# FFN gate and up of a hybrid encoder layer by seven products of halves in place of eight

## The chip, the cores and the metric

The kernel runs on one core of one Trainium2 chip. The metric is the device time in microseconds of one execution. Before: a median of 2740.31 us over 3 runs (2740.05 to 2740.49).

## What is computed

One encoder layer on 512 tokens of width 2048, in float32: a Hyena branch (long convolution) and a grouped-query attention branch, gated and merged, an output projection, and a SwiGLU feed-forward block of width 5632. The change touches the last two steps:

```python
    x = x + merged @ w_out
    h2 = rms_norm(x, ffn_norm_g)
    return x + (jax.nn.silu(h2 @ w_ffn_gate) * (h2 @ w_ffn_up)) @ w_ffn_down
```

## The kernel before

Activations lie with channels on the 128 partitions and the 512 tokens on the free axis, so a layer's input is 16 tiles of 128x512. Every weight product is taken in three matmuls (`mm3`): weights and activations are split exactly into a high and a low part, and high x high, low x high and high x low are added in one PSUM bank of 128x512. Weights come from one packed array in tiles of eight 128x128 blocks (512 KB), in the order of `weight_blocks`. `wblk` loads a tile on SP's queue (L152), casts its high part on ScalarE (L153) and subtracts it on VectorE for the low part (L154). There are 2 buffers of raw tiles and 3 each of highs and lows. All matmuls are recorded in L104, in program order; the order on the other engines is made by a scheduler.

`group` sums one 128-row output tile over its input tiles. The output projection runs 16 groups o; each adds the input (L689), and splits x2 times the norm's gain into x2h and x2l (L692, L693); `sumsq_add` gathers the squares. The norm's factor per token is not applied to x2: `token_rstd` makes it (rs2) as queued side work between matmuls and spreads it over the partitions in rbc, and gate and up are multiplied by it. Its chain is four matmuls rs2ss, a square root on ScalarE, some small VectorE steps, rs2dg, and four matmuls rs2bcp.

The feed-forward block goes in three chunks of the 44 tiles of 128 hidden channels (`DOWN`). For each tile a gate group fg and an up group fu of 48 matmuls each are followed by two scalings, Silu, a product and a split into act (L715 to L719, L176); after each chunk, 16 groups d of the down projection are added to x2 in SBUF (L725), and after the last the result is stored (L727).

Of the kernel before, what the change touches and what calls it, by code (L numbers as in the profile page):

```python
# [829 lines left out]
```

## Time and profile before

| | |
|---|---|
| median of 3 runs | 2740.31 us |
| span of the profiled execution, first to last instruction | 2738.6 us |
| TensorE busy | 2726.2 us, 12358 matmuls |
| weight loads busy (beside the matmuls) | 2250.8 us |
| VectorE busy | 1119.4 us |
| ScalarE busy | 789.8 us |
| read from HBM | 257.90 MB |

The profiled execution is one run with the hardware profiler on. A row of a group reads: line, engine, operation, written tile, read tiles, shapes, count, then busy time, mean length of one in ns, and the engine's idle time just ahead of them with what ended it. A row of a timeline reads: start and length in us, engine, line, operation, tiles, and in brackets the idle time ahead of it. The matmul records overlap, since matmuls are pipelined; what a matmul costs is the distance from start to start. A row of windows reads: the stretch, its length, then busy time and count for TensorE, weight loads, VectorE, ScalarE and GpSimd, the granted TensorE clock, the DMA share and GB/s. PEld is the weight load, SPq and ACTq are queues that issue DMAs.

### The profile page before, as it was taken

To read this page: it belongs to the slowest core of one execution; us is meant where nothing else is said; L and a number is where in the kernel's file an instruction comes from. 1 tells how busy PE (TensorE), PEld (TensorE's weight loads), DVE (VectorE), ACT (ScalarE), POOL (GpSimd) and SP (SyncE) were. 2 spreads that over 40 slices of the span, in tenths; PEclk is the share of its full clock that TensorE was granted. 3 is DMA by queue.
4 is the path that set the end of the run, shared out by engine and by line. 5 is a ranking of instruction groups with operands and counts; after the bars stand their busy time and mean duration, and the time that the engine had idled before them with its cause. 6 is when DMAs were issued, how large, how long until landed. Compare 5 with 4: busy or idle time off the path is not lost.

```text
span 2738.6 us, 29658 instructions
## 1 busy us (share of the span) xinstructions
PE 2726.2 (100%) x12358; PEld 2250.8 (82%) x12358; DVE 1119.4 (41%) x1520; ACT 789.8 (29%) x1098; POOL 34.7 (1%) x70
## 2 busy tenths in 40 slices
PE   9999999999999999999999999999999999999999
PEld 7777888888888888888888888888888888888887
DVE  7666654675333334434333332323333332333332
ACT  6333323565222223233222221222222212222221
POOL 0000001110000000000000000000000000000000
PEclk9999999999999999999999999999999999999999
...
GB/s 201 79 71 72 66 62 112 70 61 63 100 94 99 98 95 100 154 100 95 97 93 100 96 96 100 93 100 94 99 98 94 100 93 100 97 96 100 92 127 96
DMA packets 77763, 264.02 MB, mean 96 GB/s; under 512 B 8667, under 2 KB 9627, under 8 KB 77628
## 3 DMA queue, kind: packets, MB, share of 16 engines
...
HBM read 257.90 MB, written 4.19 MB: 96 GB/s over the span
## 4 chain that ended last, share of the span: by engine, by line
PE 98%; DVE 1%; ACT 1%; DMA 0%; issue 0%; SPq 0%; DVEq 0%
PE fg L104 17%; PE fu L104 17%; PE d L104 17%; PE g L104 13%; PE px L104 7%; PE o L104 6%; PE b L104 6%; PE phv L104 3%; PE q L104 2%; PE kv L104 2%; PE kp L104 2%; PE ab L104 1%; PE up L104 1%; PE av L104 1%; PE sp L104 1%; PE fp L104 1%
## 5 line engine op out<-in xcount | busy, mean ns | idle before, releaser
L153 ACT CAST wh<-wr 128x1024 fp32r<-128x1024 f32 (+1 forms) x467 | 489.4, 1049 | 1661.5 <-PE d L104 369.1
L154 DVE TENSOR_TENSOR wl<-wr,wh 128x1024 fp32r<-128x1024 f32 (+1 forms) x467 | 568.2, 1217 | 800.1 <-ACT wh L153 799.3
L104 PE MATMUL fu<-x2h,wh 128*128 128x512 f32 x704 | 274.0, 389 | 0.0
L104 PE MATMUL fg<-x2h,wh 128*128 128x512 f32 x704 | 274.0, 389 | 0.0
L104 PE MATMUL fu<-x2h,wl 128*128 128x512 f32 x704 | 273.9, 389 | 0.0
L104 PE MATMUL fg<-x2h,wl 128*128 128x512 f32 x704 | 273.9, 389 | 0.0
L104 PE MATMUL fg<-x2l,wh 128*128 128x512 f32 x704 | 273.9, 389 | 0.0
L104 PE MATMUL fu<-x2l,wh 128*128 128x512 f32 x704 | 273.9, 389 | 0.0
L104 PE MATMUL g<-xh,wh 128*128 128x512 f32 x512 | 200.4, 391 | 0.0
L104 PE MATMUL g<-xh,wl 128*128 128x512 f32 x512 | 199.4, 390 | 0.0
L104 PE MATMUL g<-xl,wh 128*128 128x512 f32 x512 | 199.4, 389 | 0.0
L104 PEld LDWEIGHTS fu<-x2l,wh 128*128 128x128 f32 x704 | 132.1, 188 | 27.5
L104 PEld LDWEIGHTS fg<-x2l,wh 128*128 128x128 f32 x704 | 132.1, 188 | 27.5
L104 PEld LDWEIGHTS fu<-x2h,wh 128*128 128x128 f32 x704 | 132.1, 188 | 27.4
L104 PEld LDWEIGHTS fg<-x2h,wh 128*128 128x128 f32 x704 | 132.1, 188 | 27.4
L104 PEld LDWEIGHTS fu<-x2h,wl 128*128 128x128 f32 x704 | 132.1, 188 | 27.4
L104 PEld LDWEIGHTS fg<-x2h,wl 128*128 128x128 f32 x704 | 132.1, 188 | 27.4
L104 PEld LDWEIGHTS g<-xh,wl 128*128 128x128 f32 x512 | 96.1, 188 | 20.1
L104 PE MATMUL px<-xh,wh 128*128 128x512 f32 x272 | 109.9, 404 | 2.5 <-ACT xh L408 1.3
L104 PEld LDWEIGHTS g<-xh,wh 128*128 128x128 f32 x512 | 96.1, 188 | 19.4
L104 PEld LDWEIGHTS g<-xl,wh 128*128 128x128 f32 x512 | 96.1, 188 | 19.2
L104 PE MATMUL px<-xh,wl 128*128 128x512 f32 x272 | 106.4, 391 | 0.5 <-DVE wl L154 0.5
...
## 6 DMA issues: line engine op xcount, KB each, us to landing
wr<-wpk SPq DMA_DIRECT2D x463, 512.0 KB, 3.3
xr<-xT SPq DMA_DIRECT2D x16, 256.0 KB, 5.6
x<-xT ACTq DMA_DIRECT2D x16, 256.0 KB, 5.2
out<-x SPq DMA_DIRECT2D x16, 256.0 KB, 2.4
dec<-decT ACTq DMA_DIRECT2D x8, 256.0 KB, 2.7
T<-tbl POOLq DMA_DIRECT2D x8, 256.0 KB, 5.1
wr<-wpk SPq DMA_DIRECT2D x4, 128.0 KB, 3.7
w<-w ACTq DMA_DIRECT2D x4, 128.0 KB, 2.6
```

The costliest lines, as they stand in the source:

```text
L104: tc.keep_in_program_order(nc.tensor.matmul(out, lhsT=lhsT, rhs=rhs, start=start, stop=stop, **kw))
L153: nc.scalar.copy(hi[:, c], raw[:, c])
L154: nc.vector.tensor_tensor(lo[:, c], raw[:, c], hi[:, c].bitcast(F32), ALU.subtract)
```

## The change

Gate and up now take two output tiles (j, j+1) of one of the two weights at a time, a group n of 44. The product is written as 2x2 halves: the weights by output tile and by even or odd input tile (a11, a12, a21, a22, each one packed tile of eight blocks), the activations by even or odd input tile and by the first or second 256 tokens. In place of eight products of halves, seven are made, of sums of halves (the Winograd form of Strassen's scheme).

- Weights: four VectorE sums a group (s1, s2, s3, s4, L775), and seven splits (cast L781, subtraction L782). Raw tiles rotate through six slots.
- Activations: once, during and behind the output projection, for each pair of input tiles the seven 256-token operands (`x_sums`) and their split (`x_split`) into X. Five of the eight pairs are made while the output projection runs, the last three behind it.
- `product`: per pair of input tiles one matmul of the weight highs with 512 columns (activation highs beside lows) and one of the weight lows with 256 columns, into the second half of the same bank. A group is 7 x 8 x 2 = 112 matmuls; the two groups that it replaces had 96.
- PSUM: banks fx (two slots), fy and fz (one each) and three others. Products are added in a bank while earlier states of it are folded out (v1, v5, v16: the halves of the bank added by ScalarE and VectorE), so a later product on the same bank waits for the fold. The order on TensorE is A11 (fx), S1 (fy), S2 (fx), S4 (fy), S3 (fx), A12 (fz), A22 (fx); in group 0 A11, A12 and S1 come first, interleaved by pairs.
- Group 0 also runs the norm's rs2ss and rs2bcp with nothing between them, between S2 and S4.
- The first four act tiles stay in SBUF, the others go to DRAM through GpSimd's queue and come back by ScalarE's queue for the down projection. x2 goes to DRAM too and is added at the end; the down sums are gathered unscaled in dacc and multiplied by rbc2 in the last chunk. Chunks are now 12, 16 and 16, and in the first chunk the first four down groups are run side by side over the act tiles.
- A small pad and a wider tile for the negated gains shift addresses, so that the large operands start at the same place in 512 bytes.

The stages ahead of the output projection have the same instructions in the same order.

```diff
-DOWN = (16, 16, 12)
+DOWN = (12, 16, 16)
+WIDE = 4
+EARLY_ACTS = 4
+NEARLY = 5
...
+    def quadrant(name, half, j):
+        return [(name, k * P, j * P, P) for k in range(half, KT, 2)]
+    for j in range(0, FT, 2):
+        for name in ("w_ffn_gate", "w_ffn_up"):
+            for half, c in ((0, 0), (0, 1), (1, 1), (1, 0)):
+                out += quadrant(name, half, j + c)
     f0 = 0
     for n in DOWN:
-        for j in range(f0, f0 + n):
-            out += cols("w_ffn_gate", j * P, KT) + cols("w_ffn_up", j * P, KT)
-        for m in range(KT):
+        first = WIDE if f0 == 0 else 0
+        for k in range(n if first else 0):
+            out += [("w_ffn_down", (f0 + k) * P, m * P, P) for m in range(first)]
+        for m in range(first, KT):
             out += cols("w_ffn_down", m * P, n, k0=f0)
...
+    r2.release()
+    r3.release()
+    H = 256
+    NP = KT // 2
+    SQ = 7 * H
+    pad = tc.alloc_tile_pool(name="pad", bufs=1, side="right")
+    pad_t = pad.tile([P, 112], F32, name="pad_t")
+    nc.vector.memset(pad_t, 0.0)
+    wq = tc.alloc_tile_pool(name="wq", bufs=1, side="right", reuse_waits="tile")
+    xa = tc.alloc_tile_pool(name="xa", bufs=1, side="right", reuse_waits="tile")
+    vp = tc.alloc_tile_pool(name="vp", bufs=1, side="right", reuse_waits="tile")
+    def ev(name):
+        return wq.tile([P, H], F32, tag="ev", bufs=6, name=name)
+    nffg = cpool.tile([P, P], F32, name="nffg")
+    nc.vector.tensor_scalar(nffg[:, :KT], prm[:, PC["ffng"]:PC["ffng"] + KT], -1.0, None, ALU.mult)
...
+    NRAW = 6
+    raws = {"n": 0, "base": None}
+    late = {}
+    def raw_tile(i, name):
+        n = raws["n"] % NRAW
+        raws["n"] += 1
+        if n < 2:
+            t = wpool.tile([P, BLK * P], F32, tag="raw", bufs=2, name=name)
+        elif n < NRAW - 1:
+            t = wq.tile([P, BLK * P], F32, tag="rb", bufs=NRAW - 3, name=name)
+        else:
+            t = late["rc"].tile([P, BLK * P], F32, tag="rc", bufs=1, name=name)
+        nc.sync.dma_start(t, wpk[i])
+        return t
...
+    def x_sums(p, xe, xo):
+        V = vp.tile([P, SQ], F32, tag="V", bufs=3, name=f"V{p}")
+        b12 = ev(f"b12{p}")
+        v = [V[:, i * H:(i + 1) * H] for i in range(7)]
+        ge, go, ngo = pcol("ffng", 2 * p), pcol("ffng", 2 * p + 1), nffg[:, 2 * p + 1:2 * p + 2]
+        nc.scalar.activation(v[0], xe[:, :H], AF.Copy, scale=ge)
+        nc.scalar.activation(b12, xe[:, H:], AF.Copy, scale=ge)
+        nc.vector.tensor_tensor(v[2], b12, v[0], ALU.subtract)
+        nc.scalar.activation(v[1], xo[:, :H], AF.Copy, scale=go)
+        nc.scalar.activation(v[5], xo[:, H:], AF.Copy, scale=ngo)
+        nc.vector.scalar_tensor_tensor(v[4], v[5], -1.0, b12, ALU.mult, ALU.subtract)
+        nc.vector.scalar_tensor_tensor(v[3], v[4], -1.0, v[0], ALU.mult, ALU.subtract)
+        nc.vector.scalar_tensor_tensor(v[6], v[3], -1.0, v[1], ALU.mult, ALU.subtract)
+        return V
+    def x_split(p, V, cuts):
+        pool = xa if p < NEARLY else late["xb"]
+        X = pool.tile([P, 2 * SQ], F32R, tag="X", bufs=NEARLY if p < NEARLY else NP - NEARLY, name=f"X{p}")
+        X4 = X.rearrange("p (i h t) -> p i h t", i=7, h=2)
+        V3 = V.rearrange("p (i t) -> p i t", i=7)
+        for a, b in zip(cuts, cuts[1:]):
+            nc.scalar.copy(X4[:, a:b, 0, :], V3[:, a:b])
+            nc.vector.tensor_tensor(X4[:, a:b, 1, :], V3[:, a:b], X4[:, a:b, 0, :].bitcast(F32), ALU.subtract)
+        xs[p] = X
+    def wsum(name, a, b):
+        t = late["sg"].tile([P, BLK * P], F32, tag="sg", bufs=3, name=name)
+        nc.vector.tensor_tensor(t, a, b, ALU.add)
+        return t
+    def wsplit(w, name):
+        hi = wpool.tile([P, BLK * P], F32R, tag="whi", bufs=3, name=f"wh{name}")
+        lo = wpool.tile([P, BLK * P], F32R, tag="wlo", bufs=3, name=f"wl{name}")
+        nc.scalar.copy(hi, w)
+        nc.vector.tensor_tensor(lo, w, hi.bitcast(F32), ALU.subtract)
+        return hi, lo
+    def product(bank, hl, i, first, p0=0, p1=NP):
+        hi, lo = hl
+        for p in range(p0, p1):
+            c = slice(p * P, (p + 1) * P)
+            x = xs[p][:, i * 2 * H:(i + 1) * 2 * H]
+            mm(bank, hi[:, c], x, first and p == 0, False, skip_group_check=True)
+            mm(bank[:, H:], lo[:, c], x[:, :H], False, p == NP - 1, skip_group_check=True)
+    def fold(name, b):
+        t = ev(name)
+        nc.scalar.copy(t, b[:, :H])
+        nc.vector.tensor_tensor(t, b[:, H:], t, ALU.add)
+        return t
...
+    def x2_tile(m, op):
+        xt = tmp(f"x2{m}")
+        nc.scalar.dma_start(xt, xT[m])
+        nc.vector.tensor_tensor(xt, op, xt, ALU.add)
+        nc.gpsimd.dma_start(x2d[m], xt)
+        return xt
+    def bank(b, n):
+        return psf.tile([P, S], F32, tag=b, bufs=2 if b == "x" else 1, name=f"f{b}{n}")
+    xt = []
+    V = {}
     for m in range(KT):
...
+        xt.append(x2_tile(m, op))
+        if m % 2:
+            p = m // 2
+            if p < NP - 1:
+                V[p] = x_sums(p, xt[m - 1], xt[m])
+            if p < NEARLY:
+                x_split(p, V[p], (0, 7))
+        if m < KT - 1:
+            sumsq_add(acc2, xt[m], m, "x2sq")
+    raws["base"] = state["tile"]
+    psm.release()
+    psf = tc.alloc_tile_pool(name="psf", bufs=1, space=PSUM, reuse_waits="tile")
+    w0 = group_raws(0)
+    h11 = wsplit(w0["a11"], "a11_0")
+    x, y, z = (bank(b, 0) for b in "xyz")
+    product(x, h11, 0, True, 0, NEARLY)
+    h12 = wsplit(w0["a12"], "a12_0")
+    product(z, h12, 1, True, 0, NEARLY)
+    r1.release()
+    late["sg"] = tc.alloc_tile_pool(name="sgp", bufs=1, reuse_waits="tile")
+    late["xb"] = tc.alloc_tile_pool(name="xb", bufs=1, reuse_waits="tile")
+    s1 = wsum("s1_0", w0["a21"], w0["a22"])
+    hs1 = wsplit(s1, "s1_0")
+    product(y, hs1, 2, True, 0, NEARLY)
+    V[NP - 1] = x_sums(NP - 1, xt[-2], xt[-1])
+    for p in range(NEARLY, NP):
+        x_split(p, V[p], (0, 3, 7))
+        product(x, h11, 0, True, p, p + 1)
+        product(z, h12, 1, True, p, p + 1)
+        product(y, hs1, 2, True, p, p + 1)
+    sumsq_add(acc2, xt[-1], KT - 1, "x2sq")
+    vp.release()
...
     rbc2 = cpool.tile([P, S], F32, tag="bc", bufs=1, name="rbc2")
...
+    def finish(n, c):
+        j, up = n // 2 * 2, n % 2
+        if not up:
+            for t in c:
+                nc.vector.tensor_tensor(t, t, rbc2, ALU.mult)
+                nc.scalar.activation(t, t, AF.Silu)
+            gated[j] = c
+            return
+        for i, (t, g) in enumerate(zip(c, gated.pop(j))):
+            nc.vector.tensor_tensor(t, t, g, ALU.mult)
+            if j + i < EARLY_ACTS:
+                act_split(j + i, t, ea, EARLY_ACTS)
+            else:
+                nc.gpsimd.dma_start(actd[j + i], t)
+    for n in range(FT):
+        if n > 0:
+            w0 = group_raws(n)
+            x, y, z = (bank(b, n) for b in "xyz")
+            product(x, wsplit(w0["a11"], f"a11_{n}"), 0, True)
+        c0, c1 = (tmp(f"c{i}_{n}") if n % 2 else cp.tile([P, S], F32, tag="c", bufs=4, name=f"c{i}_{n}")
+                  for i in range(2))
+        v1 = fold(f"v1_{n}", x)
+        if n > 0:
+            s1 = wsum(f"s1_{n}", w0["a21"], w0["a22"])
+            product(y, wsplit(s1, f"s1_{n}"), 2, True)
+        v5 = fold(f"v5_{n}", y)
+        s2 = wsum(f"s2_{n}", s1, w0["a11"])
+        product(x, wsplit(s2, f"s2_{n}"), 3, False)
+        v16 = fold(f"v16_{n}", x)
+        if n == 0:
+            for _ in token_rstd(acc2, "rs2", {"bc": rbc2}):
+                pass
+        s4 = wsum(f"s4_{n}", s2, w0["a12"])
+        product(y, wsplit(s4, f"s4_{n}"), 5, False)
+        nc.vector.tensor_tensor(v16, v16, y[:, :H], ALU.subtract)
+        nc.vector.tensor_tensor(c0[:, H:], v16, y[:, H:], ALU.subtract)
+        s3 = wsum(f"s3_{n}", w0["a11"], w0["a21"])
+        product(x, wsplit(s3, f"s3_{n}"), 4, False)
+        nc.vector.tensor_tensor(v5, v5, x[:, :H], ALU.subtract)
+        nc.vector.tensor_tensor(c1[:, H:], v5, x[:, H:], ALU.subtract)
+        if n > 0:
+            product(z, wsplit(w0["a12"], f"a12_{n}"), 1, True)
+        nc.vector.tensor_tensor(v1, z[:, :H], v1, ALU.add)
+        nc.vector.tensor_tensor(c0[:, :H], z[:, H:], v1, ALU.add)
+        product(x, wsplit(w0["a22"], f"a22_{n}"), 6, False)
+        d = ev(f"d_{n}")
+        nc.scalar.activation(d, x[:, :H], AF.Copy, scale=-1.0)
+        nc.vector.tensor_tensor(c1[:, :H], d, x[:, H:], ALU.subtract)
+        finish(n, (c0, c1))
...
+    def act_load(j, pool, bufs):
+        t = tmp(f"actr{j}")
+        nc.scalar.dma_start(t, actd[j])
+        act_split(j, t, pool, bufs)
+    dacc = [None] * KT
+    def down(ci, f0, n, m, dp, done=False):
+        last = ci == len(DOWN) - 1
+        if ci == 0:
+            dacc[m] = r3.tile([P, S], F32, tag="r", bufs=16, name=f"dacc{m}")
+        if last:
+            x2t = tmp(f"x2r{m}")
+            nc.scalar.dma_start(x2t, x2d[m])
+            nc.vector.tensor_tensor(dacc[m], dacc[m], rbc2, ALU.mult)
+            nc.vector.tensor_tensor(dacc[m], dacc[m], x2t, ALU.add)
+        if not done:
+            group(dp, [acts[j] for j in range(f0, f0 + n)])
+        if ci == 0:
+            nc.scalar.copy(dacc[m], dp)
+        elif not last:
+            nc.vector.tensor_tensor(dacc[m], dacc[m], dp, ALU.add)
+        else:
+            t = tmp(f"dt{m}")
+            nc.vector.tensor_tensor(t, dp, rbc2, ALU.mult)
+            nc.vector.tensor_tensor(dacc[m], dacc[m], t, ALU.add)
+            nc.sync.dma_start(out[m], dacc[m])
...
+        if ci == 0:
+            for j in range(EARLY_ACTS, n):
+                act_load(j, r1, NA)
+            dps = [ps_tile(f"d0{m}") for m in range(WIDE)]
+            for k in range(n):
+                for dp in dps:
+                    wh, wl = wblk()
+                    mm3(dp, wh, wl, acts[k][0], acts[k][1], k == 0, k == n - 1)
+            for m in range(WIDE):
+                down(ci, f0, n, m, dps[m], True)
+        elif ci == 1:
+            for p in (ea, xa, wq):
+                p.release()
+            r1e = tc.alloc_tile_pool(name="r1e", bufs=1, side="right", reuse_waits="tile")
+            for j in range(f0, f0 + n):
+                act_load(j, r1e, 24)
+        else:
+            for j in range(f0, f0 + n):
+                act_load(j, r1e if j < f0 + 8 else r1, 24 if j < f0 + 8 else NA)
+        for m in range(WIDE if ci == 0 else 0, KT):
+            down(ci, f0, n, m, ps_tile(f"d{ci}{m}"))
         f0 += n
```

More of the change, by code (lines that the diff above doesn't have):

```diff
@@ new lines, in fold, with group_raws @@
+    def fold(name, b):
[3 more added lines that the diff above has]
+        return t
+    def group_raws(n):
+        b = raws["base"] + 4 * n
+        t = {}
+        for q, name in ((0, "a11"), (3, "a12"), (1, "a21"), (2, "a22")) if n == 0 else \
+                ((0, "a11"), (1, "a21"), (2, "a22"), (3, "a12")):
+            t[name] = raw_tile(b + q, f"{name}_{n}")
+        return t
+    def bank(b, n):
+        return psf.tile([P, S], F32, tag=b, bufs=2 if b == "x" else 1, name=f"f{b}{n}")
@@ L684, in layer_kernel @@
+    xt = []
+    V = {}
     for m in range(KT):
[L685 to L686 removed]
+        if m == KT - 1:
+            raws["base"] = state["tile"]
         op = ps_tile(f"o{m}")
         group(op, ms)
[L689 to L692 removed]
@@ new lines, in layer_kernel, with act_tile, act_split @@
+    late["rc"] = tc.alloc_tile_pool(name="rcp", bufs=1, reuse_waits="tile")
+    cp = tc.alloc_tile_pool(name="cp", bufs=1, reuse_waits="tile")
+    ea = tc.alloc_tile_pool(name="ea", bufs=1, side="right", reuse_waits="tile")
+    rbc2 = cpool.tile([P, S], F32, tag="bc", bufs=1, name="rbc2")
+    acts = {}
+    def act_tile(j, pool, bufs):
+        t = pool.tile([P, 2 * S], F32R, tag="act", bufs=bufs, name=f"act{j}")
+        acts[j] = (t[:, :S], t[:, S:])
+        return acts[j]
+    def act_split(j, src, pool, bufs):
+        hi, lo = act_tile(j, pool, bufs)
+        nc.scalar.copy(hi, src)
+        nc.vector.tensor_tensor(lo, src, hi.bitcast(F32), ALU.subtract)
@@ new lines, in layer_kernel, with ps_tile @@
+    state["tile"] = raws["base"] + 4 * FT
+    state["pos"] = BLK
+    for p in (cp, late["rc"], late["xb"], late["sg"]):
+        p.release()
+    psf.release()
+    psd = tc.alloc_tile_pool(name="psd", bufs=1, space=PSUM, reuse_waits="tile")
+    def ps_tile(name):
+        return psd.tile([P, S], F32, tag="ps", bufs=8, name=name)
+    r3 = tc.alloc_tile_pool(name="r3d", bufs=1, reuse_waits="tile")
+    r1 = tc.alloc_tile_pool(name="r1d", bufs=1, reuse_waits="tile")
+    NA = DOWN[0] - EARLY_ACTS
@@ L706, in layer_kernel @@
     f0 = 0
     for ci, n in enumerate(DOWN):
-        acts = []
-        for j in range(f0, f0 + n):
-            gp = ps_tile(f"fg{j}")
-            group(gp, x2g)
-            up = ps_tile(f"fu{j}")
-            group(up, x2g)
-            gt = tmp(f"fgt{j}")
-            nc.vector.tensor_tensor(gt, gp, rbc2, ALU.mult)
-            nc.scalar.activation(gt, gt, AF.Silu)
-            ut = tmp(f"fut{j}")
-            nc.vector.tensor_tensor(ut, up, rbc2, ALU.mult)
-            nc.vector.tensor_tensor(ut, ut, gt, ALU.mult)
-            acts.append(split(r1, ut, "hi", "lo", 16, 16, f"act{j}"))
@@ L721, in layer_kernel @@
-        flush()
-        for m in range(KT):
-            dp = ps_tile(f"d{ci}{m}")
-            group(dp, acts)
-            nc.vector.tensor_tensor(x2[m], x2[m], dp, ALU.add)
-            if ci == len(DOWN) - 1:
-                nc.sync.dma_start(out[m], x2[m])
+        if ci == 0:
[10 more added lines that the diff above has]
+            for p in (ea, xa, wq):
+                p.release()
+            r1e = tc.alloc_tile_pool(name="r1e", bufs=1, side="right", reuse_waits="tile")
[4 more added lines that the diff above has]
+                act_load(j, r1e if j < f0 + 8 else r1, 24 if j < f0 + 8 else NA)
```

38 lines of the change are left out of this document (17 added, 21 removed).

## The prediction, made before the changed kernel was run

> **What bounds the kernel now.** I read the page first: its span, the busy lines and the chain that ended last.
>
> ```profile
> span 2738.6 us, 29658 instructions
> PE 2726.2 (100%) x12358; PEld 2250.8 (82%) x12358; DVE 1119.4 (41%) x1520; ACT 789.8 (29%) x1098; POOL 34.7 (1%) x70
> ...
> PE fg L104 17%; PE fu L104 17%; PE d L104 17%; PE g L104 13%; PE px L104 7%; PE o L104 6%; PE b L104 6%; PE phv L104 3%; PE q L104 2%; PE kv L104 2%; PE kp L104 2%; PE ab L104 1%; PE up L104 1%; PE av L104 1%; PE sp L104 1%; PE fp L104 1%
> ```
>
> TensorE is never idle, and fg and fu, the gate and up stage that the change rewrites, are 34% of the chain. Next, the windows view over 30 gate and up groups of 48 matmuls each:
>
> ```profile
> 1320.35:1646.75 326.40, 326.40 (x1441) 270.27 (x1441) 112.31 (x120) 80.49 (x91) 0.00 (x0) 1.00 0.29 97
> ```
>
> 326.40 / 30 = 10.88 us a group, 10.88 / 48 = 226.7 ns a matmul, at a granted clock of 1.00. The 88 groups take 957.4 us. VectorE is busy 112.31 / 326.40 = 34% there, so it has room; the change spends it. The groups by form give the durations:
>
> ```profile
> L154 DVE TENSOR_TENSOR wl<-wr,wh 128x1024 fp32r<-128x1024 f32 x463 | 566.7, 1224 | 799.4 <-ACT wh L153 798.6
> L153 ACT CAST wh<-wr 128x1024 fp32r<-128x1024 f32 x463 | 488.0, 1054 | 1660.4 <-PE d L104 369.1 <-PE fg L104 328.0 <-issue 236.6
> ...
> L104 PEld LDWEIGHTS fu<-x2h,wh 128*128 128x128 f32 x704 | 132.1, 188 | 27.4
> ...
> L359 ACT ACTIVATE K<-kp,prm 128x256 f32<-128x256 f32 x16 | 7.6, 474 | 55.9 <-PE kp L104 55.9
> ...
> L373 DVE TENSOR_TENSOR m<-up,K 128x256 f32<-128x256 f32 x16 | 6.6, 415 | 0.0
> ```
>
> **The new matmuls.** A product is 8 pairs of one matmul with 512 moving columns and one with 256, every one with its own weight load. The question is what a 256 costs. The timeline has a run of twelve of them, each with its own load:
>
> ```profile
> 187.63 0.28 PE L104 MATMUL up<-zt10h,T 128*128 128x256 f32 x1
> ...
> 188.94 0.28 PE L104 MATMUL up<-zt11h,T 128*128 128x256 f32 x1
> 189.06 0.40 PE L104 MATMUL px<-xh,wh 128*128 128x512 f32 x1
> 189.30 0.40 PE L104 MATMUL px<-xl,wh 128*128 128x512 f32 x1
> ```
>
> Start to start (189.06 - 187.63) / 12 = 0.119, taken as 120 ns; the 188 ns of a load row are then mostly hidden or overlapped. A pair is 226.7 + 120 = 346.7 ns, a product 2.773 us, a group of seven 19.41 us; 44 groups are 854.2 us against 957.4: **-103.2 us**. Bounds: if a 256 cost exactly half a 512, 113 ns, a pair is 340 and the term -119.6; if the 512 behind a 256 took the 235 ns that stand between 189.06 and 189.30, a pair is 355 and the term -82.8. I keep 346.7, since it is what the run itself shows.
>
> The Trainium skill, in "TensorE: Matmul & The Clock Gate" under "LDWEIGHTS (loading the stationary operand)", puts a load at the number of columns over 1.2 GHz, 107 ns here. By that the load would hide behind a 256 of 113 ns, and the term would be -119.6. The 120 ns cadence above does not agree, and it decides.
>
> **The steady loop on VectorE.** A group's vector work is eleven 1024-wide operations (four sums, seven splits), ten 256-wide ones and two of 512. What one costs its queue, and what a hand-over costs, shows in two more timelines:
>
> ```profile
> 1602.61 0.39 PE L104 MATMUL fu<-x2l,wh 128*128 128x512 f32 x1
> 1602.84 0.39 PE L104 MATMUL fu<-x2h,wl 128*128 128x512 f32 x1
> 1603.06 0.39 PE L104 MATMUL fg<-x2h,wh 128*128 128x512 f32 x1
> 1603.08 1.05 ACT L153 CAST wh<-wr 128x1024 fp32r<-128x1024 f32 x1 [4.39 <-PE fu L104]
> 1603.27 0.69 DVE L718 TENSOR_TENSOR fut<-fu,rbc 128x512 f32<-128x512 f32 x1 [3.31 <-PE fu L104]
> 1604.60 1.22 DVE L154 TENSOR_TENSOR wl<-wr,wh 128x1024 fp32r<-128x1024 f32 x1
> 1605.74 0.68 DVE L176 TENSOR_TENSOR act13l<-fut,act13h 128x512 fp32r<-128x512 f32 x1
> ```
>
> ```profile
> 14.72 1.23 DVE L154 TENSOR_TENSOR wl<-wr,wh 128x1024 fp32r<-128x1024 f32 x1 [0.81 <-ACT wh L153]
> 16.00 0.19 PEld L104 LDWEIGHTS px<-xh,wl 128*128 128x128 f32 x1 [0.96 <-DVE wl L154]
> 16.11 0.19 PEld L104 LDWEIGHTS px<-xh,wh 128*128 128x128 f32 x1
> ```
>
> A 1024 holds the queue 1.14 us (1604.60 to 1605.74) though it lasts 1.22, an overlap of 0.08; so a 256 holds it 0.34. The sum is 11 x 1.14 + 10 x 0.34 + 2 x 0.61 = 17.2 us, near 18 with operations that wait for the one before: under the 19.41 of TensorE, by little. A vector reader of a product starts 0.20 us after the product's last issue (1603.27 - 1603.06); the buffer of weight highs is free 0.47 after the start of its last use (1603.08 - 1602.61), in the new pattern 0.12 after the product's end. TensorE runs 0.16 after a vector result (15.95 to 16.11), since its load was held too.
>
> The order of the vector queue decides which folds come in time. Before, in the gate and up stage (fg and fu the gate and up accumulators, wl the weight lows):
>
> ```order
> L154 TENSOR_TENSOR wl213_10159<-wr213_10157,wh213_10158 128x1024
> L718 TENSOR_TENSOR fut2_10119<-fu2_10055,rbc2_9701 128x512
> L719 TENSOR_TENSOR fut2_10119<-fut2_10119,fgt2_10116 128x512
> L154 TENSOR_TENSOR wl214_10190<-wr214_10188,wh214_10189 128x1024
> L176 TENSOR_TENSOR act2l_10123<-fut2_10119,act2h_10122 128x512
> L154 TENSOR_TENSOR wl215_10220<-wr215_10218,wh215_10219 128x1024
> ```
>
> Now, from the split for product S4 of group 10 on (s are weight sums, v1, v5 and v16 the folds of banks fx and fy):
>
> ```order
> L782 TENSOR_TENSOR wls4_10_11824<-s4_10_11821,whs4_10_11823 128x1024
> L796 TENSOR_TENSOR v1_10_11768<-fx10_11743,v1_10_11768 128x256
> L775 TENSOR_TENSOR s1_11_11954<-a21_11_11920,a22_11_11922 128x1024
> L775 TENSOR_TENSOR s2_11_11979<-s1_11_11954,a11_11_11918 128x1024
> L796 TENSOR_TENSOR v5_10_11793<-fy10_11744,v5_10_11793 128x256
> L782 TENSOR_TENSOR wls3_10_11848<-s3_10_11845,whs3_10_11847 128x1024
> ```
>
> Before, the queue held only splits with time in hand; now the fold v1, for which product S2 waits, stands behind a split, and v5, for which S4 waits, behind two sums of the next group.
>
> (Operations of other widths than those quoted are scaled from the 1024 and 256 rows.) Count from the end of product A11 (0). Product S1 runs to 2.77; S2 writes A11's bank and needs v1. The cast for S4 takes the buffer that A11 freed: 0.12 to 1.17; its split 1.20 to 2.42; v1's copy on ScalarE 1.09 to 1.56; v1 on VectorE 2.34 to 2.76; S2 goes at 2.92: **0.15 us late**. Then s1 from 2.68, s2 (it reads s1) 3.93 to 5.15, v5 5.07 to 5.49: S4 may go at 5.65, S2 ends at 5.69, in time. v16 ends at 8.11 for an S4 that ends at 8.46; the fold before A22 ends at 12.30 for an A12 that ends at 14.00. The next A11's end comes at 19.54, with VectorE free from 20.29 and the next split due at 20.74. So 0.15 a group, 43 x 0.15 = **+6.5 us**. If each were in time: 0. If VectorE held its queue for full durations (0.08 x 2 more ahead of v1, and some ahead of v5) 0.3 to 0.5 more a group, +13 to +22.
>
> One load matters: s1 of group n+1 reads a22, whose slot is freed by s3 of group n, which ends at 18.17, that is 1.37 before the next A11's end; s1 is due 2.68 behind it, a budget of 4.05 us.
>
> ```profile
> wr<-wpk SPq DMA_DIRECT2D x463, 512.0 KB, 3.3
> xr<-xT SPq DMA_DIRECT2D x16, 256.0 KB, 5.6
> x<-xT ACTq DMA_DIRECT2D x16, 256.0 KB, 5.2
> w<-w ACTq DMA_DIRECT2D x4, 128.0 KB, 2.6
> ```
>
> A weight load lands in 3.3: covered, cost nothing. SP's queue holds a12 behind it, which is due 4 us later.
>
> **Group 0.** The tail of the output projection was followed at once by fg. Now three products run on five early pairs while VectorE adds x2, sums and splits weights and the last three pairs. From the end of o (0): x2 to 0.89, s1 to 2.03, X5 to 4.04, the split of s1 to 5.18; product S1 ran out of work at 3.47 and goes on at 5.34; X7's first part at 9.1, so the three products end at 10.3 (unhindered 8.3). Behind stand X7's rest, v1, v5, s2 (12.65), s4, and the split of s2 15.27: product S2 ends at 17.98 against 11.09, 6.9 late. The norm's matmuls come next:
>
> ```order
> L117 MATMUL fx0_9835<-X7_9917,wls2_0_9953 128x256
> L117 MATMUL rs2ss_9975<-prm_75,acc2_8650 128x1 x4
> L117 MATMUL rs2bcp_9997<-rs2dg_9992,rs2ones_9990 128x128 x4
> L117 MATMUL fy0_9836<-X0_8792,whs4_0_10005 128x512
> L117 MATMUL fy0_9836<-X0_8792,wls4_0_10006 128x256
> ```
>
> Before, the two stood in the same TensorE queue 24 matmuls apart, as here:
>
> ```order
> L104 MATMUL rs2ss_9760<-prm_73,acc2_8566 128x1 x4
> L104 MATMUL fg0_9702<-x2h15_9694,wh201_9734 128x512
> L104 MATMUL fg0_9702<-x2l15_9695,wh201_9734 128x512
> L104 MATMUL fg0_9702<-x2h15_9694,wl201_9735 128x512
> L104 MATMUL fu0_9785<-x2h0_8631,wh202_9787 128x512
> ```
>
> Nothing lies between them now, so what they waited for under cover stands on the path (a row of the chain of waits, then rows of the timeline):
>
> ```profile
> 1306.93 0.79 PE rs2ss L104 x8
> ...
> 1303.09 1.28 ACT L183 ACT_TABLE_LOAD   x1
> 1307.94 0.21 ACT L183 ACTIVATE rs2rt<-rs2a 128x4 f32<-128x4 f32 x1 [3.57 <-DVE rs2a L215]
> 1309.19 0.88 DVE L221 TENSOR_SCALAR rs2dg<-ident,rs2ry 128x128 f32<-128x128 f32 x4
> ```
>
> The table load and root end at 21.0; in the vector queue among the norm's small steps stand s1, s2 and s4 of group 1 and a split, with s1 waiting for a load issued at 16.4 that lands at about 20.0; rs2dg is done at 26.7, and rs2bcp goes at 26.9 in place of 18.8, when rs2ss with its 0.79 is through: 8.1. Without a product between them, A22 waits for the fold of S3: 1.2. Together 6.9 + 8.1 + 1.2 = **+16 us**; 8 if the norm's steps slip ahead of the sums, 25 if loads land in 5.6.
>
> In the early stage TensorE idled over a microsecond at an unchanged clock:
>
> ```profile
> 6.00:9.00 3.00, 1.68 (x7) 0.94 (x5) 1.32 (x4) 1.86 (x4) 0.00 (x0) 1.00 0.93 294
> ```
>
> The Trainium skill, in "TensorE: Matmul & The Clock Gate" under "What's actually happening", has the clock halved after an idle window of about 3.4 us, until as long a busy one. By that group 0's two longer gaps would cost some 3.4 us more, an estimate from that page. No row here has such a gap, and I leave it out.
>
> **Down.** Its matmuls stay the same. At the first block, bank x of group 43 is free 1.28 after the last product, with 0.68 of cover: 0.6. Act tiles now come back by DMA. In chunk 0, four early acts cover 10.9 us. At chunk 1, five act tiles are split ahead and eleven come through the five tmp buffers in four serial rounds behind ScalarE's casts; at 2.6 us a landing the last is about 5 us late, at 5.2 about 15, and 0 if they overlap: +5. The tail has one vector operation more behind the last matmul:
>
> ```profile
> 2734.78 0.69 DVE L725 TENSOR_TENSOR x<-x,d 128x512 f32<-128x512 f32 x1 [7.47 <-PE d L104]
> ```
>
> +0.7. Together **+6.3 us**. The sums and splits of x2 during the output projection, four 256s at 0.42 and a 1792-wide split at about 1.9, so some 3.6 us per two o groups of 10.9, hide behind o's matmuls.
>
> **Sum.** -103.2 + 6.5 + 16 + 6.3 = -74.4. The profiled execution's 2738.6 becomes 2664.2; the median of the runs, 2740.3, lies 1.7 above it: **2666 us**.
>
> **Rivals.** *Slower: the weight load inside the vector queue.* If a22 lands later than 4.05 us, s1 holds up v5 and with it S4, in every group. From 4.05 + 74.4 / 43 = 5.8 us on, the kernel is slower than before; at 6.4 us it is 2.35 x 43 = 101 us worse than forecast, 2767. For it speaks that two 512 KB loads are now issued together and that rows of 5.2 and 5.6 exist; against it, the 3.3 of 463 such loads. 7%. *Vector slip:* each group loses 0.5 to 1 us more because VectorE, 92% full, has no reserve: 2666 + 0.75 x 43 = 2698. For it, the 0.04 us to spare ahead of S4; against, the half microsecond at the group's end. 13%. *No loss:* pairs at 340 ns and folds in time: 2666 - 16.4 - 6.5 = 2643. For it, half of 226.7; against, the cadence of 120. 12%. That the products are not made is excluded by the order, which has 112 matmuls a group. The forecast has 68%, 2650 to 2690 by its own.
>
> A measurement of this kernel tells about 0.2% from no change, 5.5 us. Faster: all but the slower rival, and 1% for the loads between 5.6 and 5.8: 0.92; same 0.01; slower 0.07. The range takes in the no-loss case and the vector slip: 2640 to 2708.
>
> **What would show it.** In the profile after: pairs of matmuls at 347 ns start to start; a gap of about 0.15 us ahead of S2 and none elsewhere in a group; a gap near 8 us ahead of rs2bcp; VectorE busy about 90% through the stage; 19.6 us a group. Wrong would be groups of over 20.5 us, pairs over 355 ns, or waits of s1 on a DMA.

## The result and the profile after

The changed kernel takes 2678.28 us (median of 4 runs, 2676.52 to 2681.34) against 2740.18 before: 0.9774 of it, 95% interval 0.976 to 0.9788. The forecast was 2666, the range 2640 to 2708. The sign and the mechanism were right; 12 of the 74 us forecast did not come.

First the page of the profile after: span, busy time, chain.

```profile
span 2674.7 us, 32746 instructions
PE 2645.5 (99%) x13062; PEld 2212.9 (83%) x13062; DVE 1643.7 (61%) x2285; ACT 998.3 (37%) x1449; POOL 65.0 (2%) x126
...
PE 94%; DVE 3%; DMA 2%; ACT 1%; issue 1%; SPq 0%; ACTq 0%; DVEq 0%
```

TensorE still sets the end, but 6% of the chain now lies on other engines and on DMAs, where it was 2% before. The windows view of 600 us in the steady stage, then the tile view of fx and of d, which bound the stage:

```profile
1500.00:2100.00 600.00, 598.10 (x3395) 516.69 (x3394) 545.47 (x698) 271.63 (x365) 16.23 (x30) 1.00 0.36 119
```

```profile
L117 PE MATMUL fx<-X,wha x704: 389/395/504, 1294.6 to 2186.2; 128*128 128x512 f32 x176
```

```profile
L117 PE MATMUL d<-act,wh x1408: 387/389/503, 2186.5 to 2669.6; 128*128 128x512 f32 x176
```

VectorE is busy 545.47 / 600 = 91%, as forecast. 3395 / 112 = 30.3 groups in 600 us are 19.8 us each, not 19.56. The whole stage takes 2186.5 - 1294.6 = 891.9 us. From the start of product A11 in each group: group 0 takes 39.1 us, groups 1 to 43 take 19.83 in the mean.

**Two cadences.** Rows of the timeline after: the first matmul of a product, and the first of the next, eight pairs later, twice.

```profile
1411.89 0.39 PE L117 MATMUL fx<-X,wha 128*128 128x512 f32 x1
...
1414.66 0.39 PE L117 MATMUL fx<-X,wha 128*128 128x512 f32 x1
...
1858.14 0.40 PE L117 MATMUL fy<-X,whs 128*128 128x512 f32 x1
...
1860.96 0.40 PE L117 MATMUL fx<-X,whs 128*128 128x512 f32 x1
```

(1414.66 - 1411.89) / 8 = 346 ns a pair, as forecast; (1860.96 - 1858.14) / 8 = 352.5. No wait lies in either. Of the 301 products of groups 1 to 43, 172 run at 346 to 347 ns inside and 129 at 352 to 354; a product keeps the cadence of the one before until a wait comes. Over all, the slow ones cost 6.5 us in this execution; in acts_slot, clock_fill and rs2_later below, whose code for these groups is the same, 146, 192 and 205 products are slow, so the figure changes from run to run. The rest of the loss in these groups, 43 x (19.83 - 19.41) - 6.5 = 11.7, is waits.

**The wait of S2**, in ScalarE's, VectorE's and TensorE's rows around the start of S2 (whs and wls at 2169.64 and 2170.72 are those for S4):

```profile
2169.50 0.39 PE L117 MATMUL fy<-X,whs 128*128 128x512 f32 x1
...
2169.64 1.05 ACT L781 CAST whs<-s 128x1024 fp32r<-128x1024 f32 x1 [0.98 <-PE fx L117]
2170.72 1.22 DVE L782 TENSOR_TENSOR wls<-s,whs 128x1024 fp32r<-128x1024 f32 x1 [0.40 <-ACT whs L781]
2171.87 0.42 DVE L796 TENSOR_TENSOR v<-fx,v 128x256 f32<-128x256 f32 x1
2172.34 0.50 PE L117 MATMUL fx<-X,whs 128*128 128x512 f32 x1
2172.68 0.28 PE L117 MATMUL fx<-X,wls 128*128 128x256 f32 x1
```

The cast waits for A11's end, the split for the cast, fold v1 stands behind the split, and S2 goes at 2172.34, 2.84 after S1's start in place of 2.77; its first 512 then takes 0.34 instead of 0.23. That is 0.16 to 0.18 a group, as forecast (0.15). The forecast's 0.16 from v1's end to S2 shows as 0.05 (2172.29 to 2172.34) and the 0.11 by which the first 512 is longer.

**Group 0.** TensorE's rows that waited, and the windows of 5 us around them (the figure behind GpSimd's 0.00 (x0) is the granted clock):

```profile
1308.36 0.80 PE L117 MATMUL fx<-X,whs 128*128 128x512 f32 x1 [3.29 <-ACT whs L781]
1309.88 0.58 PE L117 MATMUL fx<-X,wls 128*128 128x256 f32 x1 [0.73 <-DVE wls L782]
...
1321.72 2.08 PE L117 MATMUL rs2bcp<-rs2dg,rs2ones 128*128 128x128 f32 x8 [6.12 <-DVE rs2dg L234]
...
1330.82 0.50 PE L117 MATMUL fx<-X,wha 128*128 128x512 f32 x1 [0.97 <-DVE c L913]
```

```profile
1305.00:1310.00 5.00, 0.98 (x3) 0.41 (x2) 5.00 (x8) 2.46 (x3) 0.00 (x0) 0.77 0.08 12
1310.00:1315.00 5.00, 5.00 (x19) 4.32 (x20) 3.56 (x4) 1.26 (x2) 0.00 (x0) 0.55 0.84 297
...
1320.00:1325.00 5.00, 3.28 (x13) 3.09 (x14) 2.15 (x8) 0.59 (x1) 0.00 (x0) 0.52 0.22 89
```

The waits are where they were forecast (ahead of S2, rs2bcp and A22), but behind the first two the granted clock falls to about half, which the sum had left out.

### The profile page after: what moved, and what is told of

Read it like the earlier page. It is cut to its first block, busy times and chain, and to the rows that moved or that the text cites. A ratio compares the mean times of both kernels' runs of the same rounds, so it can differ in the third digit from the quotient of the medians.

```text
span 2674.7 us, 32746 instructions
## 1 busy us (share of the span) xinstructions
PE 2645.5 (99%) x13062; PEld 2212.9 (83%) x13062; DVE 1643.7 (61%) x2285; ACT 998.3 (37%) x1449; POOL 65.0 (2%) x126
## 4 chain that ended last, share of the span: by engine, by line
PE 94%; DVE 3%; DMA 2%; ACT 1%; issue 1%; SPq 0%; ACTq 0%; DVEq 0%
PE d L117 17%; PE fx L117 17%; PE g L117 13%; PE fy L117 8%; PE px L117 7%; PE o L117 7%; PE b L117 7%; PE fz L117 4%; PE phv L117 3%; PE q L117 2%; PE kv L117 2%; PE kp L117 2%; PE ab L117 1%; PE up L117 1%; PE av L117 1%; PE sp L117 1%
## 5 line engine op out<-in xcount | busy, mean ns | idle before, releaser
L167 DVE TENSOR_TENSOR wl<-wr,wh 128x1024 fp32r<-128x1024 f32 (+1 forms) x291 | 352.5, 1212 | 445.4 <-ACT wh L166 443.0
L117 PE MATMUL d<-act,wh 128*128 128x512 f32 x1408 | 435.8, 390 | 2.0 <-DVE act L864 1.5
L117 PEld LDWEIGHTS d<-act,wh 128*128 128x128 f32 x1408 | 264.3, 188 | 60.7 <-DVE act L864 3.8
L781 ACT CAST whs<-s 128x1024 fp32r<-128x1024 f32 x176 | 185.3, 1053 | 255.8 <-PE fx L117 126.3
L117 PE MATMUL d<-act,wl 128*128 128x512 f32 x704 | 273.9, 389 | 0.0
L117 PE MATMUL fx<-X,whs 128*128 128x512 f32 x704 | 256.5, 404 | 5.1 <-ACT whs L781 3.3
L117 PE MATMUL fy<-X,whs 128*128 128x512 f32 x704 | 251.7, 397 | 1.9 <-DVE v L796 1.8
L117 PE MATMUL fx<-X,wha 128*128 128x512 f32 x704 | 248.5, 396 | 1.0 <-DVE c L913 1.0
L782 DVE TENSOR_TENSOR wls<-s,whs 128x1024 fp32r<-128x1024 f32 x176 | 215.0, 1222 | 25.1 <-ACT whs L781 19.8
L781 ACT CAST wha<-a 128x1024 fp32r<-128x1024 f32 x132 | 139.0, 1053 | 223.6 <-PE fx L117 106.3
L117 PE MATMUL fx<-X,wls 128*128 128x256 f32 x704 | 197.7, 281 | 0.7 <-DVE wls L782 0.7
L117 PE MATMUL fy<-X,wls 128*128 128x256 f32 x704 | 196.8, 280 | 1.3 <-DVE wls L782 1.3
L782 DVE TENSOR_TENSOR wla<-a,wha 128x1024 fp32r<-128x1024 f32 x132 | 161.3, 1222 | 12.3 <-ACT wha L781 5.2
```

Of the source, the lines that this page charges most:

```text
L117: tc.keep_in_program_order(nc.tensor.matmul(out, lhsT=lhsT, rhs=rhs, start=start, stop=stop, **kw))
L167: nc.vector.tensor_tensor(lo[:, c], raw[:, c], hi[:, c].bitcast(F32), ALU.subtract)
L781: nc.scalar.copy(hi, w)
L782: nc.vector.tensor_tensor(lo, w, hi.bitcast(F32), ALU.subtract)
```

## The experiments

Each kernel is the changed one with the edit shown. Medians of their runs, and from each trace the time from A11 to A11 and from the first to the last matmul of the down stage (2111 x 0.2267 = 478.5 without waits):

| kernel | median us | group 0 | groups 1 to 43, mean | down |
|---|---|---|---|---|
| changed | 2678.3 | 39.10 | 19.83 | 483.3 |
| clock_fill | 2674.1 | 35.73 | 19.86 | 483.9 |
| rs2_later | 2674.9 | 36.13 | 19.85 | 483.4 |
| a11_ahead | 2687.7 | | 20.08 | 483.7 |
| acts_slot | 2672.4 | 39.35 | 19.80 | 478.5 |
| v1_first | 2853.9 | 41.76 | 23.85 | 482.9 |
| hi_then_lo | 2668.1 | 40.64 | 19.56 | 483.4 |
| no_s4 | 2687.4 | 39.79 | 19.99 | 483.9 |
| pad_off | 2682.4 | 39.01 | 19.72 | 492.8 |
| whi4 | 2685.8 | 41.85 | 19.88 | 481.4 |
| best | 2653.4 | 31.17 | 19.58 | 478.5 |
| best_fill | 2659.7 | 37.28 | 19.56 | 478.5 |
| best_places | 2657.8 | 31.23 | 19.67 | 478.5 |

### Group 0: the clock and the norm

```diff
+        if n == 0:
+            fill("fill0", 16)
         product(x, wsplit(s2, f"s2_{n}"), 3, False)
...
             for _ in token_rstd(acc2, "rs2", {"bc": rbc2}):
-                pass
+                fill("fill1", 28)
```

> Sixteen matmuls of 512 columns into a spare bank (nobody reads it) stand ahead of product S2 of group 0, and twenty-eight between rs2ss and rs2bcp; nothing else is changed. If the granted clock is halved by the two idle stretches of group 0, it now stays at 1.00 there, S2 of group 0 takes 3 to 4.3 us instead of 6.2, the eight rs2bcp matmuls 0.8 instead of 2.1, group 0 some 4 to 6 us less than 39.1, and the kernel 4 to 6 us less than 2678. Rival: S2 is slow because its operands come late; then S2 stays near 6 us and the time is the same.

The windows of clock_fill at the same places:

```profile
1310.00:1315.00 5.00, 4.55 (x28) 4.05 (x29) 4.94 (x7) 2.05 (x4) 0.00 (x0) 1.00 0.77 269
...
1320.00:1325.00 5.00, 5.00 (x32) 4.49 (x31) 1.89 (x3) 2.30 (x3) 0.00 (x0) 1.00 0.21 58
```

The clock stays at 1.00 and group 0 is 39.10 - 35.73 = 3.4 us shorter, a little less than the 4 to 6 expected. Work that does nothing shortens the kernel, so the idle stretches themselves cost at least these 3.4. They cost some 1 us more, an estimate: the fillers ran to 1320.43, while rs2dg started at 1319.01, and in the changed kernel rs2bcp follows that start by 0.34.

```diff
-            for _ in token_rstd(acc2, "rs2", {"bc": rbc2}):
-                pass
+            rs2 = token_rstd(acc2, "rs2", {"bc": rbc2})
+            next(rs2)
...
         product(x, wsplit(w0["a22"], f"a22_{n}"), 6, False)
+        if n == 0:
+            for _ in rs2:
+                pass
```

> rs2bcp moves from ahead of product S4 to behind product A22 of group 0. If the norm's chain between its two groups of matmuls is what stood on the path, the 8.9 us between the last matmul of S2 and the first of S4 in group 0 shrink to under 1.5 us and the kernel is 6 to 9 us shorter, near 2670. Rival: VectorE's backlog of sums and splits sets the pace there; then groups 0 to 2 together take as long as now (80.2 us) within 2 us, with the waits in other places.

Groups 0 and 1 took 36.13 + 19.50 against 39.10 + 20.79, 4.3 less, where the first theory gave 6 to 9. The long gap is gone; another has come in TensorE's rows of rs2_later, and the clock falls again:

```profile
1317.02 0.77 PE L117 MATMUL fy<-X,whs 128*128 128x512 f32 x1
...
1326.22 0.50 PE L117 MATMUL fx<-X,wha 128*128 128x512 f32 x1 [2.08 <-DVE c L913]
```

```profile
1325.00:1330.00 5.00, 3.78 (x13) 3.25 (x14) 4.57 (x9) 0.15 (x1) 0.00 (x0) 0.67 0.00 0
```

S4 follows S2 at once (1317.02 instead of 1323.45), but A22 waits 2.08 instead of 0.97 for the fold of S3, which VectorE reaches late, and runs at half clock. So the norm's chain was on the path, and VectorE's backlog stood right behind it.

### The steady loop: load or order

```diff
+        if n + 1 < FT:
+            nxt = lead(n + 1)
         product(x, wsplit(w0["a22"], f"a22_{n}"), 6, False)
```

> Product A11 of the next group goes ahead of product A22 of this one on TensorE, so that two products lie between A11 and S2, which waits for A11's fold v1. If that wait (and the slower cadence of 353.9 ns a pair that follows a wait) is what a group loses over 19.41 us, S2's excess goes, a group takes 19.42 to 19.65 us instead of 19.83, and the kernel is 8 to 17 us shorter. Rival: VectorE, busy 90%, sets the pace; then the wait moves to another product, the group stays at 19.8 and the time at 2678 within 3 us.

(`lead` makes the loads, the split and product A11 of the next group.) Neither: a group became 0.25 longer. VectorE's rows of a11_ahead:

```profile
1700.28 1.23 DVE L782 TENSOR_TENSOR wls<-s,whs 128x1024 fp32r<-128x1024 f32 x1 [1.46 <-ACT whs L781]
1701.43 0.41 DVE L929 TENSOR_TENSOR c<-d,fx 128x256 f32<-128x256 f32 x1
1701.76 0.42 DVE L796 TENSOR_TENSOR v<-fx,v 128x256 f32<-128x256 f32 x1
```

v1's input was ready a product earlier, but in the queue it still stands behind the split for S4, and that split idles 1.46 us for a cast whose buffer now comes free with A22's end. The next run turned the order round.

```diff
-        v1 = fold(f"v1_{n}", x)
+        v1 = fold(f"v1_{n}", x, True)
...
-        product(y, wsplit(s4, f"s4_{n}"), 5, False)
+        product(y, wsplit(s4, f"s4_{n}", True), 5, False)
```

> The fold v1 is put ahead of the cast and split for product S4 in the queues of ScalarE and VectorE, in every group; with it the scheduler puts fold v5 there too. Nothing else changes, VectorE's work is the same. If S2 is late because v1 stands behind that split (in the run with A11 ahead it stood there still, behind a split that waited for a later cast), S2's excess (7.7 us over 43 groups) and S1's (4.5) go, a group takes 19.45 to 19.65 us instead of 19.83, and the kernel is 8 to 14 us shorter than 2678. Rival: VectorE, busy 90%, sets the pace; then the split for S4, now last in the row, makes S4 late instead, and the group stays at 19.8.

(With True, the two operations are kept in program order.) S1 fell to 2.80 in the mean, so S2 came in time; but the step from S2 to S4 grew to 4.37 and from S4 to S3 to 5.21. ScalarE's rows and the groups by form of v1_first show why:

```profile
1796.82 0.37 ACT L798 COPY v<-fy 128x256 f32<-128x256 f32 x1 [2.46 <-PE fy L117]
1799.64 0.37 ACT L798 COPY v<-fx 128x256 f32<-128x256 f32 x1 [2.44 <-PE fx L117]
1799.91 1.99 ACT L781 CAST whs<-s 128x1024 fp32r<-128x1024 f32 x2
```

```profile
L775 DVE TENSOR_TENSOR s<-a,a 128x1024 f32<-128x1024 f32 x88 | 107.5, 1221 | 46.8 <-DMA a<-wpk 46.8
```

The casts for S4 and S3 now stand behind copies that wait for the ends of S1 and S2, and s1, ahead of them on VectorE, waits for its load. The same work in another order costs 2853.9 - 2678.3 = 176 us. Not all of that is waiting. Ahead of S4, TensorE waits 1.41 us for the highs and 0.76 for the lows, and in 37 of the 43 groups the granted clock then falls to half: S4 takes 5.41 us in the mean there, but 3.92 in the six groups at full clock. That is 55 of the 176 us. Windows of v1_first over S4 in groups 19 and 20:

```profile
1777.80:1781.21 3.41, 2.94 (x10) 2.56 (x10) 3.41 (x4) 1.05 (x2) 0.00 (x0) 0.50 0.00 0
1801.00:1804.40 3.40, 2.64 (x13) 2.11 (x14) 3.40 (x3) 1.85 (x2) 0.00 (x0) 1.00 0.00 0
```

```diff
-        s4 = wsum(f"s4_{n}", s2, w0["a12"])
+        s4 = wsum(f"s4_{n}", s2, w0["a12"]) if n == 0 else s2
```

> The weight sum s4 is left out in groups 1 to 43 (product S4 takes s2 in its place), so VectorE has 1.14 us less to do in each and is busy 85% instead of 91%. If the order of the queue and not VectorE's load makes S2 late, S2 stays as late as it is (its mean 2.9 to 2.96 us), and the kernel is 0 to 4 us shorter. Rival: VectorE's load is the limit; then a group falls from 19.83 towards 19.45 us and the kernel by 10 us or more.

The windows view of no_s4:

```profile
1500.00:2100.00 600.00, 597.49 (x3370) 513.80 (x3369) 512.62 (x662) 269.53 (x361) 16.21 (x30) 1.00 0.36 119
```

VectorE is busy 85% and the group is longer, 19.99: less load did not shorten it, and neither 0 to 4 us nor 10 us came off the kernel. With one operation less the scheduler also made another order, so this run alone does not clear VectorE, and where the 0.16 comes from stays open. The run best below clears it: there VectorE is busy 536.63 / 600 = 89% and TensorE has no gap.

### The order inside a product

```diff
             mm(bank, hi[:, c], x, first and p == 0, False, skip_group_check=True)
+        for p in range(p0, p1):
+            c = slice(p * P, (p + 1) * P)
+            x = xs[p][:, i * 2 * H:(i + 1) * 2 * H]
             mm(bank[:, H:], lo[:, c], x[:, :H], False, p == NP - 1, skip_group_check=True)
```

> Within a product all eight matmuls of 512 columns come first, then all eight of 256. Two cadences are seen now, 346.6 and 353.9 ns a pair, and a product keeps to one of them until a wait comes. If they belong to the alternation of 512 and 256, undisturbed products now all take the same time, 8 x (226.7 + 119) = 2.77 us or a little less, and the products at 2.83 go: 2 to 6 us shorter. Rival: a run of 256s is bound by its weight loads at 120 to 130 ns, and a product takes 2.8 us or more: the same time or up to 15 us longer.

Rows of hi_then_lo: TensorE's A11 and S1, then the cast and split for S4 and fold v1.

```profile
1806.57 2.00 PE L117 MATMUL fx<-X,wha 128*128 128x512 f32 x8
1808.41 1.12 PE L117 MATMUL fx<-X,wla 128*128 128x256 f32 x8
1809.36 2.00 PE L117 MATMUL fy<-X,whs 128*128 128x512 f32 x8
...
1812.15 2.00 PE L117 MATMUL fx<-X,whs 128*128 128x512 f32 x8
```

```profile
1808.66 1.05 ACT L781 CAST whs<-s 128x1024 fp32r<-128x1024 f32 x1 [0.40 <-PE fx L117]
...
1809.75 1.23 DVE L782 TENSOR_TENSOR wls<-s,whs 128x1024 fp32r<-128x1024 f32 x1
1810.89 0.42 DVE L799 TENSOR_TENSOR v<-fx,v 128x256 f32<-128x256 f32 x1
```

The buffer of A11's highs comes free after its eight 512s: the cast starts 0.70 before S1 instead of 0.14 behind its start, v1 ends at 1811.31, 0.84 ahead of S2's start at 1812.15, and every step from product to product is 2.79. The 256s cost (1809.36 - 1808.41) / 8 = 119 ns each. The Trainium skill, "TensorE: Matmul & The Clock Gate", "LDWEIGHTS (loading the stationary operand)", gives 107 ns for a load, which would hide behind a 256 of 113; the trace does not agree, 119 to 120. The 512s cost (1808.41 - 1806.57) / 8 = 230 ns, not 226.7, so 41 of 43 groups take 19.55 and not 19.41; the cause stays open. The kernel is 10 us shorter, more than the 2 to 6 expected, since the wait went too, though group 0 is 1.5 longer; the two gains (no wait, no slow cadence) cannot be told apart in this run. The next one tries the buffer alone.

```diff
-EARLY_ACTS = 4
+EARLY_ACTS = 3
...
-        V = vp.tile([P, SQ], F32, tag="V", bufs=3, name=f"V{p}")
+        V = vp.tile([P, SQ], F32, tag="V", bufs=2, name=f"V{p}")
...
-        hi = wpool.tile([P, BLK * P], F32R, tag="whi", bufs=3, name=f"wh{name}")
+        hi = wpool.tile([P, BLK * P], F32R, tag="whi", bufs=4, name=f"wh{name}")
```

> The split weights' highs have four buffers instead of three, with the matmuls of a product alternating as in the change; to make room, the sums V have two buffers and chunk 0 three early act tiles. The cast for S4 then no longer waits for A11's last matmul. If S2 is late because that cast, the split behind it and so the fold v1 start only when A11's buffer comes free (with all 512s first it came free about 1 us earlier, and the wait was gone), S2's wait goes here too, S1 and S2 fall to 2.77 to 2.85 us in the mean, a group takes 19.45 to 19.65 us, and the gate and up stage behind group 0 is 8 to 16 us shorter; group 0 itself may be up to 5 us longer by the missing buffer of V. Rival: what was gained with all 512s first came from the cadence of that order alone; then S2 stays at 2.95 and a group at 19.8.

As a whole the expectation failed: the groups take 19.88 in the mean, and the kernel is 7.5 us slower than the changed one, 2.8 of it in group 0. In 22 of 43 groups the wait is gone (S1 2.77 to 2.83, S2 2.77 to 2.83); in most of the others S1 is 3.02 to 3.18. The difference is the order: with the fourth buffer the scheduler puts the sum s1 ahead of v1 in up groups, as VectorE's rows of whi4 show, while in gate groups v1 still follows the split.

```profile
1622.40 1.22 DVE L775 TENSOR_TENSOR s<-a,a 128x1024 f32<-128x1024 f32 x1
1623.54 0.42 DVE L796 TENSOR_TENSOR v<-fx,v 128x256 f32<-128x256 f32 x1
```

Where there is no wait, a group takes 19.41 in six cases, which is the forecast's clean group to the hundredth, and 19.78 in sixteen: all seven products at the slow cadence. So where the order stayed the buffer was the cause of the wait, and the cadence is a loss of its own, here 12.1 us. What puts TensorE into the slow one was not settled.

### Places

```diff
-    pad_t = pad.tile([P, 112], F32, name="pad_t")
+    pad_t = pad.tile([P, 104], F32, name="pad_t")
```

> The pad is 32 bytes shorter, so that five of the eight activation tiles X, three raw weight slots and the small fold tiles no longer start at the same place in 512 bytes as the split weights, the sums and the other three X. Theory: the place makes no difference to any operation here; the pair stays at 347 to 354 ns, the 1024-wide vector operation at 1.22 us, and the time at 2678 within 3 us. Rival: places that differ cost time in the engines; then the 1024-wide operations or the pairs with those X are longer and the kernel 10 us or more slower.

Both theories fell. VectorE's operations kept 1.22 us, but TensorE's cadence moved. Windows of 100 us inside the down stage, the changed kernel first, then pad_off:

```profile
2200.00:2300.00 100.00, 100.00 (x443) 82.84 (x442) 24.71 (x21) 27.57 (x33) 0.00 (x0) 1.00 0.35 115
```

```profile
2200.00:2300.00 100.00, 100.00 (x437) 81.80 (x436) 23.23 (x20) 27.49 (x33) 0.00 (x0) 1.00 0.33 110
```

443 matmuls become 437, with no wait in either: the down stage is 9.5 us longer. In gate and up all pairs run at 348 to 350 ns, between the two cadences, and that stage is 4.8 us shorter. So in this kernel a shift of 32 bytes moved a stage by 5 to 10 us, of either sign.

### The chunk of act tiles

```diff
-                act_load(j, r1e, 24)
+                act_load(j, r1e, 21)
```

> The pool into which chunk 1's act tiles are split has 21 slots instead of 24, so that none lies over the four early act tiles that chunk 0 reads to its end (chunk 2 takes other slots). If the late act tiles of chunk 1 are the 4.7 us that the down stage takes over its matmuls, all sixteen are split during chunk 0, the gaps of chunk 1 are gone, and the kernel is 4 to 5 us shorter. Rival: the loads, now beside chunk 0's weight loads, hold up acts or weights of chunk 0 by as much; then the time is the same.

Windows at the start of chunk 1, the changed kernel and acts_slot:

```profile
2317.00:2337.00 20.00, 17.98 (x69) 12.09 (x68) 11.72 (x16) 10.95 (x17) 0.00 (x0) 1.00 0.75 229
```

```profile
2317.00:2337.00 20.00, 20.00 (x90) 16.57 (x89) 8.60 (x10) 5.63 (x8) 0.00 (x0) 1.00 0.49 169
```

69 matmuls become 90, and the stage is 4.8 us shorter. The cause was one slot: the first cast of chunk 1 was to write over an early act tile, and behind it in ScalarE's queue waited the rest. In the changed kernel none of chunk 1's act casts runs before 2312; in acts_slot they run from 2201 on.

### Together

> Together: all 512s ahead of the 256s in a product, rs2bcp behind A22 in group 0, sixteen filler matmuls ahead of S2 in group 0, and 21 slots for chunk 1's act tiles. If the gains lie in different stages they add up: 10 for the products, 4.8 for the act tiles, 4 to 9 for group 0 (its clock and the norm's chain): 2655 to 2660 us. Rival: group 0's gains overlap or are lost to VectorE's backlog in group 1; then 2661 to 2664.

> As the run best, but rs2bcp stays ahead of S4, with sixteen fillers ahead of S2 and twenty-eight between rs2ss and rs2bcp to hold the clock. If moving the norm is worth more than the clock alone, this one is 1 to 4 us slower than best: 2658 to 2662. Rival: the wait that the moved norm uncovers, A22 on the fold of S3, takes it all; then both are the same within 1 us.

> As the run best, with the pad 32 bytes shorter as in pad_off, but two further pads of 32 bytes put the act tiles of the down stage back to the place in 512 bytes that the split weights have; so only five of the eight X and the raw weights and folds stand elsewhere. If the 9.5 us that the down stage lost in pad_off were the places of its act tiles, it is back at 478.5 us; and if a run of 512s slows down by places as the down's did (from 227 to 231 to 235 ns), a product takes 2.81 to 2.84 us and a group 19.7 to 19.9 instead of 19.55: 2659 to 2669 us. Rival: in gate and up the places mattered only to the alternation of 512 and 256; then a group stays at 19.55 and the time at 2653.

best takes 2653.35 us (2652.34 to 2653.67), 0.9679 of the kernel before, interval 0.9665 to 0.9694, and 24.9 less than the changed kernel, a little better than the 2655 to 2660 expected. By stages: group 0 7.9, groups 1 to 43 11.0, down 4.8. Its steady window:

```profile
1500.00:2100.00 600.00, 600.00 (x3439) 528.05 (x3438) 536.63 (x706) 277.39 (x369) 17.30 (x32) 1.00 0.36 122
```

TensorE has no gap in it. best_fill is 6.3 slower: its group 0 takes 6.1 more and group 1 1.0 less, so beside a clock that is held ahead of S2 moving the norm is worth about 5 us. In best, A22 of group 0 still waits 2.57 us for the fold of S3 and then runs at half clock; that is left. best_places is 4.5 slower: the down stage is whole again with its act tiles put back, and a group is 19.65 instead of 19.55, so places cost in a run of 512s too, about 0.1 a group.

## Why the forecast held, and where it missed

| term | forecast | measured |
|---|---|---|
| matmuls at 346.7 ns a pair | -103.2 | -103.2, and +6.5 for pairs at the slow cadence |
| waits in groups 1 to 43 | +6.5 | +11.7 |
| group 0 | +16 | +18.1 (39.10 - 19.41 - the norm's own 1.58) |
| down and tail | +6.3 | +5.5 (4.8 and 0.7) |
| sum | -74.4 | -61.4 |

The span fell by 63.9; of the other 2.5, 1.9 are the stages ahead, whose end came that much earlier in this execution. The median lies 3.6 above this span (1.7 before): the profiled run was the fastest of four, which spread over 4.8 us where the kernel before spreads over 0.7.

*Matmuls.* The pair was right to 0.1 ns for 172 products of 301, in part by luck: from start to start a 512 takes 231.2 ns in them and a 256 115.5, where the sum had 226.7 and 120, and the two misses cancel. The step was wrong in taking one cadence for all. The bound of 355 ns, read from the 235 ns of a single 512 behind a 256, lay near the other cadence, in which a 512 takes 236.4 and a 256 117.0.

*The steady loop.* S2's wait was right, cause and size: 43 x 0.16 = 6.8. hi_then_lo removed it by an earlier cast, and whi4 with a fourth buffer in the groups whose order stayed; a11_ahead and v1_first show that it hangs on the queue's order. The term as a whole was mis-sized, 11.7 for 6.5. Two things had been left out. Groups 1, 2 and 4 lose 2.2 us more, S1 to S2 taking 3.5 to 3.6: in groups 2 and 4 two splits of early act tiles stand ahead of v1, as VectorE's rows after show for group 2 (act, L864):

```profile
1357.21 0.69 DVE L864 TENSOR_TENSOR act<-c,act 128x512 fp32r<-128x512 f32 x1
...
1358.57 1.23 DVE L782 TENSOR_TENSOR wls<-s,whs 128x1024 fp32r<-128x1024 f32 x1
1359.71 0.68 DVE L864 TENSOR_TENSOR act<-c,act 128x512 fp32r<-128x512 f32 x1
1360.31 0.42 DVE L796 TENSOR_TENSOR v<-fx,v 128x256 f32<-128x256 f32 x1
```

And 2.7 us are lost in seven groups (14, 16, 20, 22, 30, 32 and 36) where S4 came late. In the same seven the sum s1 waits for its load, the one that the slower rival named:

```profile
L775 DVE TENSOR_TENSOR s<-a,a 128x1024 f32<-128x1024 f32 x88 | 107.2, 1219 | 3.5 <-DMA a<-wpk 3.3
```

```profile
a<-wpk SPq DMA_DIRECT2D x176, 512.0 KB, 4.0
```

Its landing is 4.0 in the median, not 3.3, against the budget of 4.05: it was late in these groups only, and the rival stayed small. VectorE at 91% was no limit (best, with 89% and no gap).

*Group 0.* S2 started earlier than forecast (13.7 against 15.2) and ended later (20.0 against 18.0), at half clock. rs2bcp was forecast 26.9 us after the end of o and went at 1321.72 - 1294.65 = 27.1. That is in part luck: rs2dg started 0.9 later than forecast, but rs2bcp did not wait for all four of them and went 0.34 behind the start of the first. In parts: S2 cost 8.9 (forecast 6.9), the gap ahead of rs2bcp 6.3 (8.1), A22's wait 1.3 (1.2; 0.97 is the gap itself), and rs2bcp and S4 at half clock 1.6, which the sum did not have. The step left out was the clock. The Trainium skill's rule in "TensorE: Matmul & The Clock Gate", "What's actually happening", for which the forecast gave an estimate of 3.4 us and left it out, was borne out in kind: clock_fill gained 3.4. That the figures are equal is chance, since the fillers themselves held rs2bcp up by some 1 us, and the clock also fell behind waits shorter than the page's 3.4: 3.29 here, 2.08 in rs2_later. Without the 3.4 the term would have been 14.7, so the waits alone were a little over-priced.

*Down.* The serial loads of chunk 1 cost 4.8, forecast 5; the tail 0.7, as forecast; the 0.6 at the first block did not come. The forecast took the slots of tmp for the cause; acts_slot shows that the loads were held by a cast that waited for a slot still being read, so the agreement in size is luck.
